# The residual addition of w_out: from a GpSimd addition and a store to an accumulating transfer onto x2 in DRAM

## The chip, the cores and the metric

The kernel runs on one core of one Trainium2 chip. A core has five instruction queues that run side by side: TensorE (PE; its weight loads are shown apart as PEld), VectorE (DVE), ScalarE (ACT), GpSimd (POOL) and SyncE (SP). SP only starts DMA transfers; here POOL starts a few of its own. Each queue runs its instructions strictly in the order in which they were laid down, and a wait for a semaphore holds everything behind it on that queue.

The metric is the device time of one execution in microseconds. The kernel before took 2776.52 us in the median of three runs (2768.33, 2776.52 and 2780.66).

## The reference

One layer of a streaming encoder for 2048 prompt rows and 8 × 16 rows of a second request group, with a model width of 1024. Cut to what the change touches:

```python
def rms_norm(x, g):
    y = x * lax.rsqrt(jnp.mean(x * x, axis=-1, keepdims=True) + EPS)
    return y * g

h = rms_norm(x, g0);  z = h @ w_in
A = band_attention(...)              # 8 heads x 64
B = mlstm(...)                       # 4 heads x 128
x = x + rms_norm(concat(rms_norm(A), sigmoid(o) * head_norm(B)) @ w_out)   # this line
x = x + rms_norm(conv_ffn(rms_norm(x)))                                    # w_up, conv, gelu gate, w_down
```

All of it is fp32. The marked line takes the mixed heads (rows × 1024), multiplies them by `w_out` (1024 × 1024), norms each row, scales by the row g1 and adds the layer's input x. Its result, called x2 below, is the input of the feed-forward block and of the last residual addition.

## The kernel before

**Tiling and stages.** The 2048 prompt rows are 16 tiles of 128 rows, and the second group, SAMPLE, is a 17th. The `w_in` product with attention and mLSTM runs up to about 1052 us, `w_out` from 1052 to 1323 us with the end of the attention mixed in, and then the feed-forward block in three parts of the hidden width (0, 1 and 2) up to 2778 us. x2 lives in DRAM, in one buffer `x2d[t]` per tile, and is read back three times: for the norm of the feed-forward block (`x2r`, L1079), and twice for later passes and the last addition (L1428, L1717).

**An fp32 product** is three matmuls of a rounded high part and a rest (`mm3`, L104 to L106): high·high, high·low, low·high. The parts come from a split: ScalarE casts the high part (L1309) and VectorE subtracts (L1310). `wu` are raw up-weights, `wuh` and `wul` their parts, `ws` sums of them.

**`project()`** (L968) does `w_out`, with the tiles in the order 0 to 7, SAMPLE, 8 to 15. For a tile t:

- `load` fetches the mixed heads into `mr` (L990). `norm` squares its attention half on ScalarE (L995), makes the row factor `att_rs` on POOL (L87, L93) and scales 128×512 on VectorE (L997); `turn_rows` transposes on TensorE (L76) and splits into `mt` on ScalarE and VectorE (L210, L211). All of that for tile t+1 is laid among the matmuls of tile t.
- `mx` is one tile of 2112 columns with the tag `wl`, of which there are two slots. `m` is its first 1024 columns, `xr` its second. SP loads x into `xr` (L1016).
- TensorE forms two halves `wo` of 512 columns (24 matmuls each), VectorE copies each out of PSUM into `m` (L1026), ScalarE squares it (L1028), and POOL makes the row factor `n_rs` (L87, L93).
- VectorE scales: `m = m · rs · g1` (L1038). POOL adds, `xr = m + xr` (L1039). SP stores `xr` to `x2d[t]` (L1040). When that store has landed, the slot is free.

The tag `wl` has other users: right after `project()`, the two slots of tiles 14 and 15 go to the low parts of the first up-weights (`wul`, written by VectorE at L1310). So VectorE's first `wul` waits for the store of tile 14.

**What sets the order.** The code is written as generators that are stepped in turn, so attention, mLSTM and `w_out` are laid down mixed. Then a scheduler with a simulated time line lays the instructions of each engine in a new order, and puts in the waits. An instruction in `tc.keep_in_program_order(...)` keeps its place on its engine relative to others so marked. Since the scheduler goes by its simulated times, a change in a few instructions can move many others.

Of the kernel before, what the change touches and what calls it, by code (L numbers as in the profile page):

```python
# [13 lines left out]
ALU = mybir.AluOpType  # L14
# [4 lines left out]
D = 1024  # L19
# [30 lines left out]
def hymba_step(ctx: ExitStack, tc: tile.TileContext, I: dict, O: dict):  # L50
    nc = tc.nc
# [8 lines left out]
    def ps_mm(name):  # L60
        return psum.tile([P, 512], F32, tag="mm", name=name)
# [10 lines left out]
    def dt_(shape, name):  # L72
        return dram.tile(shape, F32, tag=name, name=name)
# [12 lines left out]
    def mean_square(ms, ssq, n, eps=EPS):  # L86
        nc.gpsimd.tensor_scalar(ms, ssq, 1.0 / n, eps, op0=ALU.mult, op1=ALU.add)  # L87

    def rsqrt_mean(ssq, n, name, eps=EPS):
        ms = small.tile([P, 1], F32, tag="ms", name=name + "_ms")  # L90
        mean_square(ms, ssq, n, eps)
        rs = small.tile([P, 1], F32, tag="rs", name=name + "_rs")
        nc.gpsimd.tensor_tensor(rs, ms, nhalf[:, 0:1], op=ALU.pow)  # L93
        return rs
# [7 lines left out]
    def mm3(out, ah, al, bh, bl, start, stop, onto=False):  # L102

        nc.tensor.matmul(out, ah, bh, start=start, stop=False, skip_group_check=onto)  # L104
        nc.tensor.matmul(out, ah, bl, start=False, stop=False, skip_group_check=onto)  # L105
        nc.tensor.matmul(out, al, bh, start=False, stop=stop, skip_group_check=onto)  # L106
# [21 lines left out]
    x2d = [dt_([P, D], f"x2d{t}") for t in range(17)]  # L128

    def x_src(t):  # L130
        return I["x_sample"] if t == SAMPLE else I["x_prompt"][t * P:(t + 1) * P, :]
# [69 lines left out]
    def rows_to_T(hrow, chunk, j, name, bank):  # L201
        w = 4 if bank is not ps_big else KT
        for q in range(KT // w):
            pt = bank(f"{name}_pt{q}")
            for k in range(w):
                transpose(pt[:, k * P:(k + 1) * P], hrow[:, (w * q + k) * P:(w * q + k + 1) * P])
            ptv = pt.rearrange("p (k t) -> p k t", k=w)
            hv = chunk[:, 0, w * q:w * q + w, j * P:(j + 1) * P]
            lv = chunk[:, 1, w * q:w * q + w, j * P:(j + 1) * P]
            nc.scalar.copy(hv, ptv)  # L210
            nc.vector.tensor_tensor(lv, ptv, hv, op=ALU.subtract)  # L211
# [4 lines left out]
    def rows_tile(tag, shape, name, dtype=F32):  # L216
        if tag == "xr":
            return rows.tile(shape, dtype, tag="xr", name=name, bufs=2)
        return pa.tile(shape, dtype, tag=tag, name=name, bufs=1)
# [750 lines left out]
    def drain():  # L970
        while any([p_.step() for p_ in pipes]):
            pass

    def project(tiles):

        ss = [SimpleNamespace(t=t) for t in tiles]

        def load(s):
            t = s.t
            if t == 8:  # L980
                drain()
                open_ffn()
            s.m = rows_tile("xr", [P, D], f"mr{t}")
            if t == SAMPLE:
                for b in range(DB):
                    own = bass.AP(atts[b].tensor, atts[b].offset, [[512, DS], [DS * 512 + DA, HA], [1, DA]])
                    nc.sync.dma_start(s.m[b * DS:(b + 1) * DS, 0:512].rearrange("p (h d) -> p h d", h=HA), own)
                nc.sync.dma_start(s.m[:, 512:D], mixs)
            else:
                nc.sync.dma_start(s.m, mixd[t // 4][:, t % 4, :])  # L990

        def norm(s):
            mt = wpool.tile([P, 2112], F32R, tag="wh", name=f"mt{s.t}", bufs=2)
            ssq = small.tile([P, 1], F32, tag="ssq", name=f"assq{s.t}")
            nc.scalar.activation(mt[:, :512], s.m[:, :512], AF.Square, accum_out=ssq)  # L995
            rs = rsqrt_mean(ssq, 512, f"att{s.t}")
            nc.vector.tensor_scalar(s.m[:, :512], s.m[:, :512], rs, None, op0=ALU.mult)  # L997
            s.mt = mt[:, :2 * D].rearrange("p (a k n) -> p a k n", a=2, k=KT)

        def turn_rows(s):  # L1000
            rows_to_T(s.m, s.mt, 0, f"mT{s.t}", ps_mm if s.t < 8 else ps_big)

        load(ss[0])
        norm(ss[0])
        yield 0.0, 0.3
        turn_rows(ss[0])
        load(ss[1])
        yield 0.9, 1.2
        for n_, s in enumerate(ss):
            t = s.t  # L1010
            nxt = ss[n_ + 1] if n_ + 1 < len(ss) else None
            if nxt:
                norm(nxt)
            mx = wpool.tile([P, 2112], F32, tag="wl", name=f"mx{t}", bufs=2)
            m, xr = mx[:, 0:D], mx[:, D:2 * D]
            nc.sync.dma_start(xr, x_src(t))  # L1016
            for hf in range(2):
                c = slice(hf * 512, hf * 512 + 512)
                acc = ps_mm(f"wo{t}_{hf}")
                for k in range(KT):  # L1020
                    mm3(acc, s.mt[:, 0, k, :], s.mt[:, 1, k, :], wo[k][0][:, c], wo[k][1][:, c],
                        start=(k == 0), stop=(k == KT - 1))
                    if k % 4 == 3:
                        yield 2.6, 0.5
                ssq = small.tile([P, 1], F32, tag="wssq", name=f"wssq{t}_{hf}")
                nc.vector.tensor_copy(m[:, c], acc)  # L1026
                idle = m[:, 512:D] if hf == 0 else s.mt[:, 0, 0:4, :].rearrange("p k n -> p (k n)")
                nc.scalar.activation(idle, m[:, c], AF.Square, accum_out=ssq)  # L1028
                if hf == 0:
                    ssa = ssq  # L1030
                    mean_square(ssa, ssq, D)
                    if nxt:
                        turn_rows(nxt)
                        if n_ + 2 < len(ss):
                            load(ss[n_ + 2])
                        yield 0.9, 1.2
            rs = rsqrt_mean(ssq, D, f"n1_{t}", ssa)
            nc.vector.scalar_tensor_tensor(m, m, rs, g1[0], op0=ALU.mult, op1=ALU.mult)  # L1038
            nc.gpsimd.tensor_tensor(xr, m, xr, op=ALU.add)  # L1039
            nc.sync.dma_start(x2d[t], xr)  # L1040

# [5 lines left out]
    def open_ffn():  # L1049

        p1.close()
        ffn.p3 = ctx.enter_context(tc.tile_pool(name="p3", bufs=2, reuse_waits="tile"))
        ffn.halo = ffn.p3.tile([P, 44, 2], F32, tag="halo", name="halo", bufs=1)
        nc.vector.memset(ffn.halo, 0.0)
        ffn.g2 = ffn.p3.tile([P, D], F32, tag="g2", name="g2", bufs=1)
        nc.sync.dma_start(ffn.g2, I["norm_g"][2:3, :].broadcast_to([P, D]))
        pipes[:] = [Pipe(h2_units(0, lead=6)), Pipe(iter([]))]
# [187 lines left out]
    for n_, (half, gi) in enumerate(seq):  # L1245
# [22 lines left out]
        if n_ == len(seq) - 1:  # L1268
            out = project([0, 1, 2, 3, 4, 5, 6, 7, SAMPLE, 8, 9, 10, 11, 12, 13, 14, 15])
            split = w_out_steps()  # L1270
            next(split)
            next(out)
# [711 lines left out]
```

## Time and profile before

| | |
|---|---|
| Runs | 2768.33, 2776.52, 2780.66 us; median 2776.52 |
| Profiled execution | 2780.55 us |
| Its span, first to last instruction | 2778.8 us |
| Mean granted TensorE clock | 0.994 |
| TensorE busy | 2700.5 us (97%) |
| VectorE busy | 1971.7 us (71%) |
| ScalarE busy | 1439.6 us (52%) |
| GpSimd busy | 658.6 us (24%) |
| Moved by DMA | 532.52 MB, mean 192 GB/s |
| Stage `w_out`, 1052 to 1323 us: TensorE, VectorE, GpSimd busy | 265.76, 192.61, 101.94 of 271 us |

How to read it: the span runs from the first to the last instruction of one profiled execution, the time lies a little above it. Busy times of engines overlap. In the timeline each row has a start, a duration, the engine, the line of the code and the tiles `out<-in`; a bracket at the end tells for how long the engine had stood idle just before and whose end released it. A granted clock of 1.00 is TensorE's full speed.

### The profile page before, as it was taken

How to read it: one execution, taken by the hardware profiler on the slowest of the kernel's cores; microseconds unless marked ns; L12 is line 12 of the kernel's file. 1: busy time of each engine (PE TensorE's matmuls, PEld its weight loads, DVE VectorE, ACT ScalarE, POOL GpSimd, SP SyncE). 2: the span in 40 equal slices, each digit the busy share in tenths (PEclk: the TensorE clock that was granted, in tenths of full speed). 3: DMA queues.
4: the chain of work that ended last, by engine and by line, in shares of the span. 5: the costliest groups of instructions: out<-in, count | busy, mean ns of one | idle time of the engine just before them, and what ended most of it. 6: DMA issues, size and time to landing. Idle time of an engine off the chain costs nothing.

```text
span 2778.8 us, 47788 instructions
## 1 busy us (share of the span) xinstructions
PE 2700.5 (97%) x16422; PEld 2525.1 (91%) x16422; DVE 1971.7 (71%) x3637; ACT 1439.6 (52%) x2918; POOL 658.6 (24%) x1249
## 2 busy tenths in 40 slices
PE   7999999999999999999999999999999999999998
PEld 7899999998899998878999998789999778989976
DVE  5244455645546668766989987668998866999966
ACT  4355555634346666543555455445455665545554
POOL 1000010211100002335433322123442112555301
PEclk9999999999999999999999999999999999999999
DMA  5534355556564456345645559866775766777775
GB/s 182 157 116 139 105 164 168 163 152 211 156 184 141 136 169 196 107 163 195 230 153 188 167 183 329 301 224 198 225 225 170 250 223 231 216 236 231 233 268 183
DMA packets 322850, 532.52 MB, mean 192 GB/s; under 512 B 59650, under 2 KB 156638, under 8 KB 322478
## 3 DMA queue, kind: packets, MB, share of 16 engines
q1 hardware_dynamic: 251838, 400.11, 46.6%
q0 software_dynamic: 25840, 83.98, 7.9%
q10 hardware_dynamic: 44928, 45.37, 5.0%
q8 instruction: 129, 2.11, 0.3%
q14 instruction: 115, 0.94, 0.1%
HBM read 383.28 MB, written 149.18 MB: 192 GB/s over the span
## 4 chain that ended last, share of the span: by engine, by line
PE 49%; DVE 5%; DMA 3%; issue 2%; ACT 1%; POOL 1%; SPq 0%; DVEq 0%; POOLq 0%; ACTq 0%
PE uec L104 5%; PE uec L105 5%; PE uec L106 5%; PE dn L106 4%; PE dn L105 3%; PE dn L104 3%; PE ua L106 3%; PE ua L105 3%; PE ua L104 3%; PE wo L106 2%; PE wo L104 2%; PE wo L105 2%; PE dnm L105 1%; PE dnm L106 1%; PE dnm L104 1%
## 5 line engine op out<-in xcount | busy, mean ns | idle before, releaser
L104 PE MATMUL uec<-B,wuh 128*128 128x384 f32 (+1 forms) x720 | 237.8, 331 | 11.8 <-DVE uu L1642 10.7
L105 PE MATMUL uec<-B,wuh 128*128 128x384 f32 (+1 forms) x720 | 236.5, 328 | 0.0
L106 PE MATMUL uec<-B,wul 128*128 128x384 f32 (+1 forms) x720 | 234.8, 328 | 0.0
L1309 ACT CAST wuh<-wu 128x512 fp32r<-128x512 f32 x255 | 141.4, 618 | 112.4 <-PE uec L105 105.4
L1310 DVE TENSOR_TENSOR wul<-wu,wuh 128x512 fp32r<-128x512 f32 x255 | 170.4, 703 | 4.0 <-DMA x2d<-mx 2.8
L405 DVE CUSTOM_DVE_ANT_0 tmp<-s,nb 128x640 f32<-128x640 f32 (+4 forms) x128 | 94.4, 738 | 95.6 <-PE s L395 94.2
L104 PE MATMUL vo<-wi_h,hT 128*128 128x256 f32 x544 | 155.2, 285 | 0.8 <-DVE mt L211 0.6
L106 PE MATMUL vo<-wi_h,hT 128*128 128x256 f32 x544 | 155.6, 286 | 0.0
L105 PE MATMUL vo<-wi_l,hT 128*128 128x256 f32 x544 | 154.8, 285 | 0.0
L104 PEld LDWEIGHTS uec<-B,wuh 128*128 128x128 f32 x720 | 136.2, 189 | 15.3 <-DVE uu L1642 12.4
L104 PE MATMUL qk<-hT,wi_h 128*128 128x384 f32 (+1 forms) x384 | 130.3, 339 | 7.4 <-ACT qk_st L236 4.1
L105 PEld LDWEIGHTS uec<-B,wuh 128*128 128x128 f32 x720 | 136.4, 189 | 0.2
L106 PEld LDWEIGHTS uec<-B,wul 128*128 128x128 f32 x720 | 136.2, 189 | 0.0
L1506 ACT ACTIVATE y<-y 128x768 f32<-128x768 f32 (+1 forms) x66 | 53.8, 815 | 155.5 <-DVE y L1504 155.5
L418 DVE TENSOR_TENSOR ptl<-pt,pth 128x640 fp32r<-128x640 f32 (+4 forms) x128 | 93.7, 738 | 56.5 <-ACT pth L417 55.5
L406 ACT ACTIVATE tmp<-tmp,mn 128x640 f32<-128x640 f32 (+4 forms) x128 | 97.6, 762 | 64.2 <-DVE mn L405 62.4
L1310 DVE TENSOR_TENSOR wdl<-wdr,wdh 128x512 fp32r<-128x512 f32 x198 | 124.9, 686 | 7.0 <-ACT wdh L1309 6.8
L105 PE MATMUL qk<-hT,wi_h 128*128 128x384 f32 (+1 forms) x384 | 128.9, 336 | 0.0
L106 PE MATMUL qk<-hT,wi_l 128*128 128x384 f32 (+1 forms) x384 | 128.5, 335 | 0.0
L1310 DVE TENSOR_TENSOR al<-ar,ah 128x768 fp32r<-128x768 f32 (+2 forms) x94 | 71.1, 765 | 80.9 <-ACT ah L1309 80.7
L105 PE MATMUL qb<-hT,wi_h 128*128 128x384 f32 (+1 forms) x384 | 127.9, 333 | 0.0
L106 PE MATMUL qb<-hT,wi_l 128*128 128x384 f32 (+1 forms) x384 | 127.2, 331 | 0.0
(443 smaller groups left out, 9443.9 us busy)
## 6 DMA issues: line engine op xcount, KB each, us to landing
wu<-in_w_up SPq DMA_DIRECT2D x220, 256.0 KB, 4.4
wu<-wsd SPq DMA_DIRECT2D x176, 256.0 KB, 4.1
wdr<-in_w_down SPq DMA_DIRECT2D x110, 256.0 KB, 5.8
wi_raw<-in_w_in SPq DMA_DIRECT2D x52, 512.0 KB, 4.0
wsd<-ws POOLq DMA_DIRECT2D x88, 256.0 KB, 3.7
wdr<-wtd SPq DMA_DIRECT2D x88, 256.0 KB, 4.8
gr<-gd SPq DMA_DIRECT2D x39, 384.0 KB, 5.9
kraw<-kTd SPq DMA_DIRECT2D x112, 128.0 KB, 3.2
```

Of the source, the lines that this page charges most:

```text
L104: nc.tensor.matmul(out, ah, bh, start=start, stop=False, skip_group_check=onto)
L105: nc.tensor.matmul(out, ah, bl, start=False, stop=False, skip_group_check=onto)
L106: nc.tensor.matmul(out, al, bh, start=False, stop=stop, skip_group_check=onto)
L405: nc.vector.tensor_tensor_reduce(o_, s_, b_, 1.0, 3e38, ALU.add, ALU.min, accum_out=mn)
L406: nc.scalar.activation(tmp[:, :n], tmp[:, :n], AF.Exp, bias=mn, scale=-1.0, accum_out=rsum[:, i % 4, hh:hh + 1])
L418: nc.vector.tensor_tensor(s.ptl[:, sl, qc], ptv, s.pth[:, sl, qc], op=ALU.subtract)
L1309: nc.scalar.copy(h, r)
L1310: nc.vector.tensor_tensor(l, r, h, op=ALU.subtract)
L1506: nc.scalar.activation(y[:, :ln], y[:, :ln], AF.Gelu_apprx_tanh)
```

## The change

The second half of `mx` is no longer used. At the start of a tile's loop SP copies x from its input straight into `x2d[t]`, in DRAM; this copy is marked to keep its place in SP's order. After VectorE's scaling there is no addition on POOL and no store on SP. Instead POOL starts one DMA transfer that adds `m`, as it lies in SBUF, onto `x2d[t]` (`accum_op=ALU.add`). It waits for the scaling and for the copy. The slot of `mx` is free when this transfer has landed, and the readers of `x2d[t]` wait for it too.

```diff
             mx = wpool.tile([P, 2112], F32, tag="wl", name=f"mx{t}", bufs=2)
-            m, xr = mx[:, 0:D], mx[:, D:2 * D]
-            nc.sync.dma_start(xr, x_src(t))
+            m = mx[:, 0:D]
+            tc.keep_in_program_order(nc.sync.dma_start(x2d[t], x_src(t)))
             for hf in range(2):
...
             rs = rsqrt_mean(ssq, D, f"n1_{t}", ssa)
             nc.vector.scalar_tensor_tensor(m, m, rs, g1[0], op0=ALU.mult, op1=ALU.mult)
-            nc.gpsimd.tensor_tensor(xr, m, xr, op=ALU.add)
-            nc.sync.dma_start(x2d[t], xr)
+            nc.gpsimd.dma_start(x2d[t], m, accum_op=ALU.add)
```

Line numbers of the new kernel are the old ones up to L1038, and one less behind it. SP has 1445 rows before and 1428 now; POOL has as many as before. The other engines have the same instructions as before, in an order that differs from the end of the attention to the first part of the feed-forward block.

On POOL, around the end of tile 9 (`n1_9_rs` is that tile's row factor, `att11_rs` that of the heads of tile 11, `mx9` its slot), before:

```order
L93 TENSOR_TENSOR n1_9_rs_15547<-n1_9_ms_15545,nhalf_77 128x1
L87 TENSOR_SCALAR att11_ms_15555<-assq11_15553 128x1
L93 TENSOR_TENSOR att11_rs_15557<-att11_ms_15555,nhalf_77 128x1
L1039 TENSOR_TENSOR mx9_15455<-mx9_15455 128x1024
L87 TENSOR_SCALAR wssq10_0_15606<-wssq10_0_15606 128x1
```

and now:

```order
L93 TENSOR_TENSOR n1_9_rs_15537<-n1_9_ms_15535,nhalf_77 128x1
L87 TENSOR_SCALAR att11_ms_15544<-assq11_15542 128x1
L93 TENSOR_TENSOR att11_rs_15546<-att11_ms_15544,nhalf_77 128x1
L1039 DMA x2d9_289<-mx9_15445 128x1024
L87 TENSOR_SCALAR wssq10_0_15595<-wssq10_0_15595 128x1
```

The transfer stands in the place of the addition, between the row factor of the next tile's heads and the next tile's mean square.

On VectorE, at the end of `w_out` (`wo14_1` is the second half of tile 14, `wul0_0_0` the first up-weights' low part, in a slot that `mx14` had), before:

```order
L1026 COPY mx14_16018<-wo14_1_16060 128x512
L1038 SCALAR_TENSOR_TENSOR mx14_16018<-mx14_16018,n1_14_rs_16090,norm_row1_13117 128x1024
L1026 COPY mx15_16095<-wo15_0_16097 128x512
L1310 TENSOR_TENSOR wul0_0_0_16167<-wu0_0_16168,wuh0_0_0_16166 128x512
L1310 TENSOR_TENSOR wul0_0_0_16167<-ws0_1_16177,wuh0_0_0_16166 128x512
L1310 TENSOR_TENSOR wul0_0_0_16167<-ws0_2_16178,wuh0_0_0_16166 128x512
L1310 TENSOR_TENSOR wul0_0_0_16167<-ws0_0_16176,wuh0_0_0_16166 128x512
L1326 TENSOR_TENSOR ws1_0_16239<-wu1_3_16237,wu1_2_16235 128x512
L1026 COPY mx15_16095<-wo15_1_16126 128x512
```

and now:

```order
L1026 COPY mx14_16003<-wo14_1_16045 128x512
L1325 TENSOR_TENSOR ws0_1_16160<-ws0_0_16159,wu0_0_16151 128x512
L1325 TENSOR_TENSOR ws0_2_16161<-wu0_0_16151,wu0_3_16157 128x512
L1325 TENSOR_TENSOR ws0_3_16162<-wu0_1_16153,ws0_1_16160 128x512
L1026 COPY mx15_16079<-wo15_0_16081 128x512
L1038 SCALAR_TENSOR_TENSOR mx14_16003<-mx14_16003,n1_14_rs_16075,norm_row1_13117 128x1024
L1026 COPY mx15_16079<-wo15_1_16110 128x512
L1309 TENSOR_TENSOR wul0_0_0_16150<-wu0_0_16151,wuh0_0_0_16149 128x512
L1309 TENSOR_TENSOR wul0_0_0_16150<-ws0_1_16160,wuh0_0_0_16149 128x512
```

The scaling of tile 14 now stands behind the first evacuation of tile 15, and the first `wul` behind the second evacuation of tile 15; the sums `ws0`, which stood further ahead, stand between the evacuations.

On SP at the same place, before (`lated` are late parts of the feed-forward block's input; `B3` reads them), in part:

```order
L1040 DMA x2d12_292<-mx12_15784 128x1024
L1016 DMA mx14_16018<-in_x_prompt 128x1024
L1115 DMA lated1_277<-b212_15994 512x1x128
L1321 DMA wu0_0_16168<-in_w_up 128x512
L1115 DMA lated2_278<-t42_15996 512x1x128
L1321 DMA wu0_1_16170<-in_w_up 128x512
L1321 DMA wu0_2_16172<-in_w_up 128x512
L1321 DMA wu0_3_16174<-in_w_up 128x512
L1040 DMA x2d13_293<-mx13_15904 128x1024
L1321 DMA wu1_0_16231<-in_w_up 128x512
L1321 DMA wu1_1_16233<-in_w_up 128x512
L1016 DMA mx15_16095<-in_x_prompt 128x1024
```

and now:

```order
L1114 DMA lated1_277<-b212_15980 512x1x128
L1320 DMA wu0_0_16151<-in_w_up 128x512
L1114 DMA lated2_278<-t42_15982 512x1x128
L1016 DMA x2d14_294<-in_x_prompt 16x8192
L1016 DMA x2d15_295<-in_x_prompt 16x8192
L1320 DMA wu0_1_16153<-in_w_up 128x512
L1320 DMA wu0_2_16155<-in_w_up 128x512
L1320 DMA wu0_3_16157<-in_w_up 128x512
L1320 DMA wu1_0_16214<-in_w_up 128x512
L1320 DMA wu1_1_16216<-in_w_up 128x512
```

No store stands between the weight loads any more, and the copies of x for the last two tiles stand together ahead of them.

## The prediction

> **What bounds the kernel now.** I read the head of the page first, then the windows of the stage that changes, what TensorE waits for there, and last the rows of the edited lines.
>
> ```profile
> span 2778.8 us, 47788 instructions
> PE 2700.5 (97%) x16422; PEld 2525.1 (91%) x16422; DVE 1971.7 (71%) x3637; ACT 1439.6 (52%) x2918; POOL 658.6 (24%) x1249
> ```
>
> TensorE is busy for 97% of the span. What any other engine saves counts only where TensorE has a gap. The `w_out` stage runs from 1052 to 1323 us, and the hand-over to the feed-forward block takes the next 23 us (columns: window, its length, then busy us of PE, PEld, DVE, ACT and POOL, granted clock, DMA share, GB/s):
>
> ```profile
> 1052.00:1323.00 271.00, 265.76 (x1424) 222.79 (x1423) 192.61 (x302) 132.55 (x315) 101.94 (x137) 0.99 0.50 163
> 1323.00:1346.00 23.00, 20.80 (x118) 19.90 (x117) 22.18 (x28) 14.10 (x21) 8.11 (x9) 1.00 0.70 267
> 1346.00:1680.00 334.00, 331.85 (x1860) 323.93 (x1859) 306.40 (x467) 171.18 (x278) 115.48 (x196) 1.00 0.55 183
> ```
>
> TensorE is idle for 271.00 − 265.76 = 5.2 us in the stage, 2.2 us in the hand-over and 2.2 us in the 334 us behind it. That is the whole visible purse. From 1052 to 1346 us its gaps end as follows (total, times, longest):
>
> ```profile
> PE pt L76 <- DVE ptl L418: 1.8, 1, 1.8
> PE ua L106 <- DVE wul L1310: 1.6, 1, 1.6
> PE ub L106 <- DVE wu L1310: 0.6, 1, 0.6
> PE ot L431 <- DVE ptl L418: 0.5, 1, 0.5
> PE wo L104 <- DVE mt L211: 0.4, 1, 0.4
> ```
>
> Every one is VectorE being late; neither the additions nor the stores of x2d end a gap.
>
> **The change, part by part.** The groups of the edited lines, and of one line beside them (duration in ns min/median/max, then first and last start):
>
> ```profile
> L1039 POOL TENSOR_TENSOR mx<-mx x17: 2373/2394/2575, 1077.2 to 1329.5; 128x1024 f32<-128x1024 f32 x17
> L1040 SPq DMA_DIRECT2D x2d<-mx x17: 319/326/397, 1079.6 to 1332.1; - x17
> L1016 SPq DMA_DIRECT2D mx<-in_x_prompt x16: 327/338/567, 1052.3 to 1310.3; - x16
> L997 DVE TENSOR_SCALAR mr<-mr,att_rs x17: 482/2604/2621, 1013.0 to 1304.1; 128x512 f32<-128x512 f32 x17
> ```
>
> *Removed: 17 additions on POOL.* 17 × 2.394 = 40.7 us of POOL. POOL is busy 102 of 271 us in the stage and ends no TensorE gap, so this by itself is 0. But look at L997: the same 128x512 scaling takes 0.48 us at least and 2.60 us in the median. The timeline shows which:
>
> ```profile
> 1175.47 2.39 POOL L1039 TENSOR_TENSOR mx<-mx 128x1024 f32<-128x1024 f32 x1
> 1175.53 2.61 DVE L997 TENSOR_SCALAR mr<-mr,att_rs 128x512 f32<-128x512 f32 x1 [0.71 <-POOL att_rs L93]
> 1178.66 0.81 DVE L405 CUSTOM_DVE_ANT_0 tmp<-s,nb 128x640 f32<-128x640 f32 x1
> 1181.58 0.83 DVE L418 TENSOR_TENSOR ptl<-pt,pth 128x640 fp32r<-128x640 f32 x1 [0.30 <-ACT pth L417]
> 1182.46 0.77 PE L76 MATMUL pt<-ident,tmp 128*128 128x128 f32 x5 [1.80 <-DVE ptl L418]
> ...
> 1240.13 0.49 DVE L997 TENSOR_SCALAR mr<-mr,att_rs 128x512 f32<-128x512 f32 x1 [0.71 <-POOL att_rs L93]
> ```
>
> The scaling that starts beside the addition at 1175.47 ends with it (1178.14 against 1177.86); the one at 1240.13, with no addition beside it, takes 0.49. So more than half of the 17 lose 2.1 us of VectorE each. Behind the long one stand the softmax's L405 and L418, and behind those the longest gap, 1.80. Without the block L405 could start about 1.4 us earlier (the evacuation between them then waits for its product for part of the 2.1). The clock columns show what such a gap costs besides:
>
> ```profile
> 1184.00:1188.00 4.00, 4.00 (x13) 3.22 (x12) 2.12 (x5) 1.60 (x5) 0.00 (x0) 0.63 0.19 79
> 1188.00:1192.00 4.00, 4.00 (x24) 3.41 (x23) 0.00 (x0) 0.00 (x0) 0.00 (x0) 1.00 0.02 4
> ```
>
> Right after it the granted clock is 0.63 for 4 us: 13 matmuls, against 24 in the next 4 us. 4 × (1 − 0.63) = 1.5 us. The gaps of 0.54 and 0.41 stand at 1160.99 and 1164.68, behind
>
> ```profile
> 1156.73 2.62 DVE L997 TENSOR_SCALAR mr<-mr,att_rs 128x512 f32<-128x512 f32 x1 [0.71 <-POOL att_rs L93]
> ```
>
> The gain is 1.4 + 1.5 + 0.5 + 0.4 = 3.8 us. Bounds: nothing, if a later link of the chain (ScalarE's exponentials) is the true limit; 5.2 + 1.5 = 6.7, if every gap of the stage goes.
>
> *Removed and added on SP.* 17 loads (0.34 each) and 17 stores (0.33) go, 17 copies of x come: one issue per tile fewer, 17 × 0.33 = 5.5 us of SP. SP's waits shrink more:
>
> ```profile
> SPq L1040 <- POOL mx L1039: 91.0, 15, 19.6
> SPq L1016 <- DMA x2d<-mx: 27.2, 12, 2.9
> ```
>
> The store's 91.0 us in line ahead of later loads move to POOL, the load's 27.2 us of waiting for the slot go. No gap of TensorE in the list ends with a load, so I take 0; a weight that arrives sooner has no one waiting for it. Cover gone, the price would be at most the 2.9 us of one such wait. The copies are pinned in SP's order, wait for no buffer, and stand a tile ahead of the accumulation that needs them. They add a read and a write that replace the load's read and the store's write; the accumulation adds 512 KB read and 512 KB written per tile: 17 MB over 271 us is 66 GB/s on 163. In the hand-over the share of the DMA engines is 0.70 already, which lengthens landings there.
>
> *Added on POOL: 17 accumulating transfers.* No row shows one. Issuing and landing are bounded by the nearest rows:
>
> ```profile
> L1328 POOL DMA_DIRECT2D wsd<-ws x88: 539/539/760, 1309.2 to 1621.7; - x88
> x2d<-mx SPq DMA_DIRECT2D x17, 512.0 KB, 3.0
> x2r<-x2d SPq DMA_DIRECT2D x17, 512.0 KB, 6.0
> wsd<-ws POOLq DMA_DIRECT2D x8, 256.0 KB, 6.5
> ```
>
> The issue costs POOL 0.54 in place of 2.39 and waits where the addition waited, for VectorE's scaling (and for the copy); behind it on POOL are the next tile's mean squares, which come sooner. Landing L: 3.0 is the plain store, a floor; two landings one after the other, 6.0 + 6.5 = 12.5, are my ceiling. I take 6.0, nearest to the row of the same 512 KB out of x2d and to POOL's own transfers in these microseconds.
>
> [...]
>
> *Moved: who frees the slot.* `mx` has two slots, so tile 15 needs tile 13's.
>
> ```profile
> 1302.10 1.28 DVE L1038 SCALAR_TENSOR_TENSOR mx<-mx,n_rs,norm_row 128x1024 f32<-128x1024 f32 x1 [1.00 <-POOL n_rs L93]
> 1317.44 0.69 DVE L1026 COPY mx<-wo 128x512 f32<-128x512 f32 x1 [1.73 <-PE wo L106]
> 1318.22 0.33 SPq L1040 DMA_DIRECT2D x2d<-mx  x1
> 1320.97 0.69 DVE L1310 TENSOR_TENSOR wul<-wu,wuh 128x512 fp32r<-128x512 f32 x1 [2.83 <-DMA x2d<-mx]
> 1323.89 0.34 PE L106 MATMUL ua<-B,wul 128*128 128x384 f32 x1
> ```
>
> The scale of tile 13 ends at 1303.4, tile 15's first evacuation starts at 1317.44: 14 us for L, so 0 by L = 6.0. At the end the cover is thinner. Tile 14's slot goes to `wul`, the first up-weights; VectorE already waits 2.83 us for the store there, and TensorE needs `wul` at 1323.89. In the new order tile 14's scaling stands behind tile 15's first evacuation, so it ends at 1317.44 + 0.69 + 1.28 = 1319.4; then L, then 0.69: 1319.4 + 6.0 + 0.7 = 1326.1, a gap of about 2.2 us. Ends: L = 3.0 gives none by this (about 0.6, since tile 15's second evacuation, for a matmul that ends at 1323.0, now also precedes `wul`); L = 12.5 gives 8.7. A gap of 1.80 cost 1.5 by the clock, one of 1.6 (in the hand-over, clock 1.00) nothing: half, 0.7. Together +2.9 (0.6 to 10.2).
>
> *Moved: the rest.* The scheduler re-laid matmuls, splits and evacuations from the attention tail through the first block. Each place can be better or worse; the nearest measure is the 2.2 us of gaps in the 334 us behind, so 0, with ends of −4 and +4 (two gaps of about 2 us either way).
>
> **Sum.** −3.8 + 2.9 + 0 = −0.9 on the profiled execution's 2780.55 (its span is 2778.8): 2779.65. That execution is 4.0 above the median of the runs, 2776.52; taken over, 2776 us (2775.6, rounded).
>
> **Rivals.** *Accumulations land too late (slower).* With L above 14 us the two slots bind. For: no row shows an accumulating transfer, and it reads DRAM and writes it back. Against: 3.0 to 6.5 in the rows. At L = 20 each slot's round, two tiles long, grows by up to 6 us, 3 us per tile over the 15 tiles that reuse a slot, up to 45; the end adds 16. With attention work filling a part, about +50: 2826. It decides from about L = 15: 15 × 0.5 for the slots, 11.2 at the end, 0.7, less 3.8, is 15.6, over the 14 us that can be told.
>
> *The new order stalls TensorE (slower).* The moved rows, not the transfer: VectorE is busy 22.18 of 23 us in the hand-over and 306 of 334 behind it, so work put ahead of a split is felt at once. Against: as many rows moved forward as back. Six more gaps of 1.8 with the clock's 1.5: 6 × 3.3 = 20 us, 2796.
>
> *VectorE freed is worth more (faster).* If the 2.1 us blocks also cost TensorE time that shows as busy, all gaps go and some hidden time: 7.4 + 1.5 + some 6 us, about −15: 2761. Against: TensorE already covers most of the dozen blocks without a gap.
>
> *The change doesn't do what it says.* If POOL's transfer waited for a late copy, or its issue cost as much as the addition, VectorE would be blocked as before: gain 0, end +2.9, 2779.4. SP's order puts the copies well ahead, so I give it little and count it under no change.
>
> **How the numbers follow.** About 0.5%, 14 us, is what a measurement of this kernel can tell from no change. My forecast, with the case just named, has 0.67 (own range 2768 to 2788); late landing 0.10; the new order 0.17; more than the gaps 0.06. So faster 0.06, same 0.67, slower 0.27. The range is 2764 to 2806: it takes in the terms' ends (−6.7 + 0.6 − 4 and 10.2 + 4), and half of the slower cases; beyond it lie about 0.15 above and 0.04 below.
>
> **What would show it.** L997 at 0.48 us in nearly all 17; no POOL addition, 17 issues near 0.54; the 1.80 gap and the 0.63 clock behind it gone; landing of the accumulations near 6 us; VectorE's first `wul` waiting for that landing, and a TensorE gap of about 2 us at 1324. Wrong would be: landings over 15 us, with evacuations L1026 waiting for them; or the same landings and many new gaps in the attention tail or the first block.

## The result and the profile after

The changed kernel takes 2795.49 us in the median of six runs, against 2777.97 for six of the kernel before: a ratio of 1.0072 (95% interval 1.0057 to 1.0087), 17.5 us slower. The forecast was "no change", 2776; the range (2764 to 2806) holds the time, the direction was missed. The profiled execution of the changed kernel took 2806.41 us, the longest of the six, so its rows are read for what waits for what, and a second profile of the same kernel (2794.17 us, the first experiment) for what comes back.

The head of the page, changed kernel:

```profile
span 2804.7 us, 47744 instructions
PE 2712.3 (97%) x16422; PEld 2535.2 (90%) x16422; DVE 1940.9 (69%) x3637; ACT 1438.0 (51%) x2918; POOL 634.1 (23%) x1249
```

VectorE and POOL did get lighter, by 31 and 24 us, and TensorE is still busy for 97%. The groups that answer to the edited lines, and L997 beside them:

```profile
L1039 POOL DMA_DIRECT2D x2d<-mx x17: 878/917/1081, 1078.7 to 1341.9; - x17
L1016 SPq DMA_DIRECT2D x2d<-in_x_prompt x16: 499/618/1266, 1055.2 to 1307.5; - x16
L997 DVE TENSOR_SCALAR mr<-mr,att_rs x17: 480/486/523, 1014.1 to 1308.7; 128x512 f32<-128x512 f32 x17
DMA to landing us min/median/max: 5.4/6.1/11.3
```

(The last line is that of the accumulating transfers.) VectorE's blocks are gone: all 17 scalings take 0.48 to 0.52 us. The median landing is 6.1 us, as forecast. What was not forecast, in size or at all, are these waits of TensorE from 1320 to 1860 us, the three longest:

```profile
PE ua L106 <- DVE wul L1309: 8.3, 1, 8.3
PE dnm L104 <- ACT gh L1308: 7.5, 4, 4.6
PE h2T_pt L1106 <- ACT b L1123: 2.0, 1, 2.0
```

**First place, the hand-over at 1323 us.** The timeline of POOL, VectorE and TensorE around tile 14:

```profile
1321.52 0.43 POOL L87 TENSOR_SCALAR n_ms<-wssq,wssq 128x1 f32<-128x1 f32 x1
1321.90 1.15 POOL L1327 DMA_DIRECT2D wsd<-ws  x2
1322.02 0.69 DVE L1026 COPY mx<-wo 128x512 f32<-128x512 f32 x1 [0.20 <-PE wo L106]
1323.06 0.58 POOL L93 TENSOR_TENSOR n_rs<-n_ms,nhalf 128x1 f32<-128x1 f32 x1
1323.68 1.29 DVE L1038 SCALAR_TENSOR_TENSOR mx<-mx,n_rs,norm_row 128x1024 f32<-128x1024 f32 x1 [0.96 <-POOL n_rs L93]
...
1325.27 0.94 POOL L1039 DMA_DIRECT2D x2d<-mx  x1 [0.25 <-DVE mx L1038]
...
1336.67 0.69 DVE L1309 TENSOR_TENSOR wul<-wu,wuh 128x512 fp32r<-128x512 f32 x1 [8.29 <-DMA x2d<-mx]
...
1337.42 0.69 PE L106 MATMUL ua<-B,wul 128*128 128x384 f32 x1 [8.30 <-DVE wul L1309]
```

VectorE is idle for 0.96 us ahead of tile 14's scaling: it waits for the row factor `n_rs`, which POOL makes 1.54 us after the mean square `n_ms`, because two transfers of weight sums (`wsd`) stand between them; in the kernel before the two rows are 0.34 us apart (1313.49 and 1313.83). Tile 14's transfer starts at 1325.27 and VectorE goes on at 1336.67: 11.4 us. In the same microseconds SP sends the four late parts of the block's input, 768 KB each:

```profile
1324.15 4.28 SPq L1163 DMA_DIRECT2D B<-lated  x4
```

The windows of the changed kernel behind that (window, length, busy us of PE, PEld, DVE, ACT and POOL, then granted clock, share of the DMA engines and GB/s):

```profile
1329.00:1333.00 4.00, 0.12 (x1) 0.00 (x0) 0.00 (x0) 1.79 (x5) 0.82 (x2) 0.99 1.03 300
1333.00:1337.00 4.00, 0.00 (x0) 0.00 (x0) 0.33 (x1) 0.00 (x0) 0.00 (x0) 0.50 1.01 377
1337.00:1341.00 4.00, 3.58 (x11) 3.58 (x12) 4.00 (x7) 0.00 (x0) 0.33 (x1) 0.50 0.26 102
1341.00:1345.00 4.00, 4.00 (x18) 4.00 (x18) 2.88 (x5) 3.98 (x5) 2.28 (x4) 0.73 0.55 176
```

The DMA engines are full, 1.03 and 1.01, while TensorE stands still. The clock is 0.50 when it goes on, and 0.73 for 4 us more, which costs another 4 × 0.50 + 4 × 0.27 = 3.1 us.

**Second place, the end of the feed-forward's first block, 340 us later.** No line of the diff is there. The timeline of ScalarE in the kernel before:

```profile
1658.56 1.03 ACT L1502 ACTIVATE y<-ug,wcv 128x768 f32<-128x768 f32 x1
1659.50 1.76 ACT L1309 CAST gh<-gr 128x384 fp32r<-128x384 f32 x4
1662.86 1.06 ACT L1095 ACTIVATE B<-x2r 128x1024 fp32r<-128x1024 f32 x1 [1.61 <-DMA x2r<-x2d]
...
1668.02 1.06 ACT L1095 ACTIVATE B<-x2r 128x1024 fp32r<-128x1024 f32 x1 [1.63 <-DMA x2r<-x2d]
```

and in the changed kernel, with one row of TensorE:

```profile
1670.21 1.06 ACT L1094 ACTIVATE B<-x2r 128x1024 fp32r<-128x1024 f32 x1 [5.77 <-DMA x2r<-x2d]
...
1673.34 1.03 ACT L1501 ACTIVATE y<-ug,wcv 128x768 f32<-128x768 f32 x1
1674.27 1.74 ACT L1308 CAST gh<-gr 128x384 fp32r<-128x384 f32 x4
...
1687.99 1.06 ACT L1094 ACTIVATE B<-x2r 128x1024 fp32r<-128x1024 f32 x1 [6.36 <-DMA x2r<-x2d]
...
1691.63 0.83 ACT L1308 CAST gh<-gr 128x768 fp32r<-128x768 f32 x1
...
1692.51 0.80 PE L104 MATMUL dnm<-wdh,gh 128*128 128x512 f32 x1 [4.55 <-ACT gh L1308]
```

The first `B<-x2r` (the square for the next block's norm) now stands ahead of the gate's `y` and of the splits `gh`, and waits 5.77 us for its load in place of 1.61. What stands behind it comes late; SP sends the second x2r load late in turn (at 1679.99, after a wait for VectorE's `y`), the second `B<-x2r` waits 6.36, and the splits that TensorE needs stand behind that one. TensorE's gap of 4.55 is followed by the clock's drop, and so is a second stretch of gaps 90 us later (windows of the changed kernel):

```profile
1690.00:1700.00 10.00, 7.49 (x21) 5.94 (x22) 6.32 (x9) 3.96 (x7) 0.69 (x2) 0.66 0.91 322
...
1780.00:1790.00 10.00, 8.90 (x31) 7.09 (x32) 9.30 (x17) 7.67 (x18) 5.42 (x11) 0.66 0.65 247
```

**How much at each place.** From windows of 20 us I added up the counts of TensorE's matmuls, and read (between two windows, in proportion) when the 7500th, the 9000th and so on had started, in each kernel's profile and in that of the kernel before. The growth of the difference from the 7500th to the 9000th (1071 to 1353 us before) is the loss in `w_out` with the hand-over, from the 10500th to the 11500th (1612 to 1828 us) that at the end of the first block. All are against one profile of the kernel before, and stretches in which no row moved differ by up to 5 us between profiles, so only large entries mean something.

| Kernel | `w_out` and hand-over, us | End of block, us | Ratio to before (95%) |
|---|---|---|---|
| changed | 13.0 | 14.2 | 1.0072 (1.0057 to 1.0087) |
| changed, again | 9.6 | 13.8 | 1.0052 (1.0033 to 1.0071) |
| tiles 14 and 15 old | 0.9 | 1.3 | 0.9999 (0.9987 to 1.0011) |
| before, with copies | 0.9 | 0.3 | 1.0001 (0.9991 to 1.0010) |
| before, no addition | −1.5 | 1.8 | 0.9987 (0.9974 to 1.0000) |
| tile 15 old | 6.3 | 1.7 | 1.0028 (1.0018 to 1.0038) |
| other buffer | 9.2 | 14.2 | 1.0058 (1.0043 to 1.0073) |
| plain transfers | 8.6 | 12.1 | 1.0054 (1.0034 to 1.0074) |
| only 14 and 15 new | −0.6 | 10.0 | 1.0044 (1.0029 to 1.0059) |
| not pinned | 0.0 | −0.4 | 1.0100 (1.0076 to 1.0125) |
| not pinned, two old | −1.1 | 0.9 | 1.0079 (1.0063 to 1.0095) |
| copy half a tile later | 10.5 | 0.5 | 1.0039 (1.0025 to 1.0053) |
| copy two tiles earlier | 2.9 | 0.3 | 1.0006 (0.9993 to 1.0018) |

The two unpinned kernels lose 22 to 26 us in the first 100 us. The experiments follow in the order in which they were run.

### The profile page after: what moved, and what is told of

The parts are those of the page before. It is cut to its first block, busy times and chain, and to the rows that moved or that the text cites. A ratio compares the mean times of both kernels' runs of the same rounds, so it can differ in the third digit from the quotient of the medians.

```text
span 2804.7 us, 47744 instructions
## 1 busy us (share of the span) xinstructions
PE 2712.3 (97%) x16422; PEld 2535.2 (90%) x16422; DVE 1940.9 (69%) x3637; ACT 1438.0 (51%) x2918; POOL 634.1 (23%) x1249
## 4 chain that ended last, share of the span: by engine, by line
PE 43%; DMA 3%; DVE 3%; issue 2%; ACT 1%; POOL 1%; SPq 0%; ACTq 0%; DVEq 0%; POOLq 0%
PE uec L104 6%; PE uec L105 6%; PE uec L106 6%; PE dn L106 3%; PE dn L105 3%; PE dn L104 3%; PE ua L106 3%; PE ua L105 3%; PE ua L104 3%; PE ub L106 1%; PE ub L105 1%; PE ub L104 1%; PE dnm L104 1%; PE dnm L106 1%; PE dnm L105 1%
```

## The experiments

Each edit is against the changed kernel unless it says otherwise. The theory after the first comparison: two costs, the wait for tile 14's accumulation at the hand-over, and the moved rows at the end of the first block. The rivals: everything is order; everything follows from the late `wul`; the accumulating transfer itself costs time wherever it stands.

**The changed kernel again** (no edit).

> The changed kernel once more, for a second profile beside the others. If the gap of 8.30 us at the first wul, which waits for tile 14's accumulation, belongs to the kernel, it is here again within 1 us, with the granted clock low behind it; time 2790 to 2798. If the two clock drops between 1680 and 1790 us belong to the order, they are here again; if they were chance, this profile has other ones and the time is nearer 2790.

2793.97 us. TensorE's gaps from 1323 to 1350, and from 1350 to 1900 us:

```profile
PE ua L106 <- DVE wul L1309: 7.3, 1, 7.3
...
PE dnm L104 <- ACT gh L1308: 5.3, 3, 4.7
PE h2T_pt L1106 <- ACT b L1123: 5.2, 1, 5.2
```

Both places come back, with the clock low behind them (0.50 from 1324 to 1332 us and 0.76 for 4 us more; 0.83 from 1680 to 1700 us), so they belong to the kernel. Of the 12 us by which the first profile was longer, some 5 lie ahead of the 7500th matmul and some 3 in `w_out` with the hand-over; they did not come back.

**Tiles 14 and 15 undone.**

```diff
-            m = mx[:, 0:D]
-            tc.keep_in_program_order(nc.sync.dma_start(x2d[t], x_src(t)))
+            m, xr = mx[:, 0:D], mx[:, D:2 * D]
+            if t in (14, 15):
+                nc.sync.dma_start(xr, x_src(t))
+            else:
+                tc.keep_in_program_order(nc.sync.dma_start(x2d[t], x_src(t)))
...
-            nc.gpsimd.dma_start(x2d[t], m, accum_op=ALU.add)
+            if t in (14, 15):
+                nc.gpsimd.tensor_tensor(xr, m, xr, op=ALU.add)
+                nc.sync.dma_start(x2d[t], xr)
+            else:
+                nc.gpsimd.dma_start(x2d[t], m, accum_op=ALU.add)
```

> Tiles 14 and 15 alone go back to the load of x, the POOL addition and the SP store; the other 15 tiles accumulate as in the changed kernel. Theory (the end: the first wul waits for an accumulation that lands late): the gap at the first wul falls from 8.3 to under 2.5 us, the clock behind it stays at 1.00, and the time falls by about 10 us against the changed kernel, to about 2786. Rival (the moved rows of w_out cost it): those rows up to the end of w_out stand as in the changed kernel, so the time stays above 2790.

2778.82 us against 2778.57 for the kernel before: the whole loss is gone, more than expected, because the order of the first block went back to the old one too. TensorE has no gap at the first `wul`; a later `wul`, some 17 us on, has one of 1.6, as in the kernel before (at 1342.62 and 1341.01). And VectorE's blocks stay away (L997 takes 0.49 us in the median, 0.53 at most), without the kernel being faster than the one before. So freeing VectorE is not worth its 3.8 us here: TensorE's idle time from 1052 to 1323 us is 271.00 − 263.67 = 7.3 us, 5.2 before, and its longest waits there have other names:

```profile
PE h2T_pt L1113 <- DVE x2r L1105: 2.4, 3, 0.9
PE wo L106 <- DVE mt L211: 2.0, 3, 1.1
PE ot L430 <- ACT pth L417: 1.1, 1, 1.1
```

**The kernel before, with the copies alone.** The edit is against the kernel before.

```diff
+            tc.keep_in_program_order(nc.sync.dma_start(x2d[t], x_src(t)))
             nc.sync.dma_start(xr, x_src(t))
```

> The kernel before with nothing but the 17 pinned copies of x onto x2d added; the later stores overwrite them. All four computing engines keep their order row by row. Both theories: within 3 us of the kernel before, 2775 to 2781, since neither SP nor DRAM ends a gap. If the copies or their place in SP's order cost time (the rival that the DMA traffic does it), 5 us or more above the kernel before.

1.0001. The copies and their place in SP's order cost nothing while the other engines' rows stand as before.

**The kernel before, without the POOL additions.** Against the kernel before.

```diff
-            nc.gpsimd.tensor_tensor(xr, m, xr, op=ALU.add)
-            nc.sync.dma_start(x2d[t], xr)
+            nc.sync.dma_start(x2d[t], m)
```

> The kernel before without the 17 POOL additions: m is stored without x, the loads of x stay. It leaves out the residual addition. It measures what freeing POOL and VectorE is worth without any accumulation: L997 at 0.49 us in all 17. By the sum of the prediction 3.8 us faster than before, about 2774; by the rival that VectorE's free time is covered by TensorE's own work, within 1.5 us of before; by the rival that the block also costs hidden time, 10 us or more faster.

2776.76 us, 1.8 us under the kernel before, with an interval from 0 to 7 us. That takes in the 3.8 as well as the second alternative, and this run does not tell them apart.

**Tile 15 alone undone.** The edit of tiles 14 and 15 with `t == 15`.

> Tile 15 alone goes back to load, POOL addition and store; tile 14 still accumulates, and its slot still goes to the first wul. Behind the hand-over all rows stand as in the kernel with tiles 14 and 15 undone. Theory of two costs (the wait for tile 14's accumulation, about 9 us; and rows of the first block put in another order, about 12 us): a gap of 5 to 9 us at the first wul with a low clock behind it, no loss between 1600 and 1860, about 2787. Rival (all follows from the late wul, which throws the later rows off): the loss between 1600 and 1860 comes too, 2793 or more. Rival (all is order): no gap, 2779.

2786.00 us: the end of the block is well (1.7), and `w_out` with the hand-over loses 6.3. But not as expected: in this order tile 14's transfer starts at 1318.21, ahead of the late parts (1323.91), and VectorE waits 1.28 us for it. The loss is another wait, VectorE for a weight load, with tile 15's rows `mt` behind it (timeline of VectorE):

```profile
1310.38 0.69 DVE L1332 TENSOR_TENSOR ws<-wu,wu 128x512 f32<-128x512 f32 x1 [6.78 <-DMA wu<-in_w_up]
```

**m of tiles 14 and 15 in another buffer.**

```diff
-            mx = wpool.tile([P, 2112], F32, tag="wl", name=f"mx{t}", bufs=2)
+            if t in (14, 15):
+                mx = row(f"mx{t}")
+            else:
+                mx = wpool.tile([P, 2112], F32, tag="wl", name=f"mx{t}", bufs=2)
```

> All 17 tiles accumulate as in the changed kernel, but m of tiles 14 and 15 lies in a row buffer of the feed-forward block, so that wul's slots come free with tiles 12 and 13. The rows from 1400 us to the end of the second block stand exactly as in the changed kernel. Theory of two costs: no wait for an accumulation at the first wul, the loss between 1600 and 1860 with its clock drops is here all the same (12 us or so), about 2789. Rival (all follows from the late wul): no loss there either, about 2779.

2794.18 us. No `wul` waits for an accumulation, and the end of the block still loses 14.2 (`gh` 6.5, `b` 5.5 us of gaps). So the second cost doesn't follow from the late `wul`. (The hand-over as a whole is still 9.2 us late here. That lateness is not the cause either: two kernels below lose at one of the two places and not at the other.) The hand-over stayed dear here by another wait, TensorE for the late part's split, 3.7 us.

**Plain transfers.**

```diff
-            nc.gpsimd.dma_start(x2d[t], m, accum_op=ALU.add)
+            nc.gpsimd.dma_start(x2d[t], m)
```

> The changed kernel with plain transfers in place of the accumulating ones, from the same POOL queue; every row of every engine stands as in the changed kernel. It leaves out the residual addition. If accumulation as such makes the landing long (a read and an add more), the median landing falls from 6.1 to about 4 us, that of tile 14 from 11 to about 6, the gap at wul from 8 to about 3 us, and the time by 5 to 9 us. If the load on the DMA engines at that place makes it (weights, the late parts B and the sums wsd land there too), tile 14's landing stays at 9 us or more and the time at 2790 to 2797.

2795.29 us, with all rows as in the changed kernel. The group of the transfers, and their landing:

```profile
L1039 POOL DMA_DIRECT2D x2d<-mx x17: 539/683/757, 1076.6 to 1334.7; - x17
DMA to landing us min/median/max: 3.0/4.3/10.6
```

TensorE's gaps at the two places:

```profile
PE ua L106 <- DVE wul L1309: 3.5, 1, 3.5
...
PE dnm L104 <- ACT gh L1308: 5.6, 3, 4.0
```

This tells two things apart. Accumulating costs 6.1 − 4.3 = 1.8 us of landing in the median, 5.4 − 3.0 = 2.4 between the shortest, and 0.23 us of issue; at tile 14 the transfer takes 7.7 us from its issue to VectorE's `wul` (1321.86 to 1329.54) against 11.4 and 10.7, and the gap is 3.5 against 8.3 and 7.3. And the end of the block loses 12.1 us without any accumulation, so that loss is the order's. The time did not fall by the 5 to 9 us expected: the median is that of the changed kernel, over a wide spread (2784.68 to 2800.87). Of the 8.6 us in the table 3.8 come ahead of the hand-over, between the 7500th and the 8000th matmul.

**Only tiles 14 and 15 new.** The edit of tiles 14 and 15, with `t not in (14, 15)`.

> The complement: only tiles 14 and 15 accumulate, the other 15 load, add and store as before. Up to the end of w_out the rows stand as in the kernel before, so POOL blocks VectorE there as before; behind it they stand nearly as in the changed kernel. If the whole loss lies with the last two tiles (the wait and the rows moved by it), the time is that of the changed kernel, 2790 to 2798, with both the gap at wul and the loss between 1600 and 1860. If the 15 others share in it, 2787 or less.

2789.24 us, in between: the end of the block loses 10.0, `w_out` with the hand-over nothing. Up to `w_out`'s end its rows are the old ones, so tile 14 is scaled before tile 15's evacuation, its transfer starts at 1312.12, 3.5 us ahead of the burst of late parts, and `wul` starts 6.7 us later:

```profile
1312.12 0.95 POOL L1046 DMA_DIRECT2D x2d<-mx  x1 [1.63 <-DVE mx L1041]
1318.86 0.69 DVE L1316 TENSOR_TENSOR wul<-wu,wuh 128x512 fp32r<-128x512 f32 x1 [4.62 <-DMA x2d<-mx]
```

The accumulation of tile 14 alone is thus not dear; it is dear where it falls into the burst. (No run moves the burst alone; this compares orders.)

**The copies not kept at their place.**

```diff
-            tc.keep_in_program_order(nc.sync.dma_start(x2d[t], x_src(t)))
+            nc.sync.dma_start(x2d[t], x_src(t))
```

> The changed kernel with the copies of x not kept at their place: the scheduler lays all 17 near the head of SP's order. In the first block ScalarE's rows then stand as in the kernel before (the down-weight splits behind gh of the fifth step), while at the hand-over tile 14's scaling and the first wul stand as in the changed kernel. Theory of two costs: a gap of 4 to 8 us at the first wul, no loss between 1600 and 1860, about 2787, if the early copies cost nothing at the start. Rival (the accumulations disturb the first block by themselves): the loss between 1600 and 1860 is there, 2793 or more.

2805.28 us, for a reason of its own: the scheduler puts the 17 copies at the head of SP's order (10.0 to 33.2 us), where TensorE waits for its first inputs, and some 25 us are lost by the 500th matmul. Its first window:

```profile
0.00:40.00 40.00, 20.83 (x115) 19.47 (x116) 14.79 (x25) 13.65 (x21) 5.00 (x23) 0.90 0.97 336
```

The DMA engines are full (0.97) and TensorE runs 115 matmuls; in the kernel before it runs 216 in that window, with the DMA engines at 0.70. Behind that, neither place loses anything (0.0 and −0.4), though all 17 tiles accumulate. The expectation was mistaken in one thing: in this order tile 14's scaling stands ahead of tile 15's evacuation, as in the kernel before, so the gap at `wul` is 0.5 us.

**The same with tiles 14 and 15 undone.** Both edits together.

> The same with tiles 14 and 15 gone back to load, addition and store: neither cost is left, VectorE is free of the POOL additions in 15 tiles. Theory: 2775 to 2780, the time of the kernel before, since the gaps that the free VectorE closes are replaced by others. If the pinned copies held something back on SP that the gain of 3.8 us needs, 2774 or less, faster than both kernels.

2800.44 us: 22 us at the start, nothing behind it. The expectation forgot the start.

**The pinned copy half a tile later.**

```diff
-            tc.keep_in_program_order(nc.sync.dma_start(x2d[t], x_src(t)))
...
                 if hf == 0:
+                    tc.keep_in_program_order(nc.sync.dma_start(x2d[t], x_src(t)))
                     ssa = ssq
```

> The whole change, all 17 tiles accumulate, but the pinned copy stands one half tile later: behind the evacuation of the tile's first half instead of at the start of its loop. The scheduler's rows of the first block then stand as in the kernel before; the hand-over stands as in the changed kernel (tile 14's scaling behind tile 15's first evacuation, the first wul last). Theory (order alone decides each cost): the wait at the first wul and its gap of 5 to 8 us are here, the loss between 1600 and 1860 isn't; 2783 to 2788. Rival (accumulation itself costs it): as the changed kernel, 2791 or more.

2788.45 us, 10 us over the kernel before: the gap at `wul` is here alone. Its gaps from 1320 to 1360 us, the longest of them:

```profile
PE ua L106 <- DVE wul L1309: 7.4, 1, 7.4
```

There is no gap of `dnm` from 1600 to 1870 us.

**The pinned copy two tiles earlier.**

```diff
                 nc.sync.dma_start(s.m, mixd[t // 4][:, t % 4, :])
+            tc.keep_in_program_order(nc.sync.dma_start(x2d[t], x_src(t)))
...
-            tc.keep_in_program_order(nc.sync.dma_start(x2d[t], x_src(t)))
```

> The whole change, all 17 tiles accumulate, but the pinned copy stands two tiles earlier, behind the load of the tile's mixed heads. Here both places stand as in the kernel before: tile 14's scaling ahead of tile 15's first evacuation, and ScalarE's rows of the first block in the old order. Theory (order alone decides each cost): no gap over 2.5 us at the first wul, no loss between 1600 and 1860, 2775 to 2781, the kernel before within 0.15%. Rival (accumulation itself costs time, wherever it stands): 2785 or more. If the freed POOL and VectorE are worth the 3.8 us of the prediction in this order, 2774 or less.

2778.94 us against 2778.46, a ratio of 1.0006. The whole change costs nothing that these runs can tell in this order (the interval is −1.9 to +5.0 us). The timeline of VectorE, TensorE and ScalarE at the two places:

```profile
1311.49 0.69 DVE L1325 TENSOR_TENSOR ws<-wu,wu 128x512 f32<-128x512 f32 x1 [6.38 <-DMA wu<-in_w_up]
1315.31 0.80 PE L106 MATMUL wo<-wo,mt 128*128 128x512 f32 x1 [3.98 <-DVE mt L211]
1317.72 1.28 DVE L1038 SCALAR_TENSOR_TENSOR mx<-mx,n_rs,norm_row 128x1024 f32<-128x1024 f32 x1 [1.88 <-POOL n_rs L93]
1323.13 0.69 DVE L1026 COPY mx<-wo 128x512 f32<-128x512 f32 x1 [4.13 <-PE wo L106]
1325.19 0.69 DVE L1309 TENSOR_TENSOR wul<-wu,wuh 128x512 fp32r<-128x512 f32 x1 [1.36 <-DMA x2d<-mx]
...
1670.99 1.06 ACT L1094 ACTIVATE B<-x2r 128x1024 fp32r<-128x1024 f32 x1 [2.28 <-DMA x2r<-x2d]
```

Tile 14 is scaled ahead of tile 15's evacuation, VectorE waits 1.36 us for the transfer, and ScalarE 2.28 us for x2r. There is one other stop, as with tile 15 alone undone: VectorE waits 6.38 us for a weight load, tile 15's rows `mt` come behind that, and TensorE stands still for 3.98 us, with a granted clock of 0.84 over the window from 1300 to 1320 us. So the 2.9 us in the table have a cause of their own. The kernel does not beat the one before, and no run here tries whether it would without that stop.

## Why the prediction was wrong, point by point

- **VectorE freed (−3.8).** The mechanism was right: L997 is 0.47 to 0.53 without an addition beside it. The size did not show: 1.8 us (0 to 7) without the additions, which leaves 3.8 possible, and nothing (0.9999, 1.0006) in the two accumulating kernels in a good order, which have new gaps of their own. The clock's price of a gap, 1.5 us, was counted as a gain, while new gaps of the same kind can pay it too. The list of gaps in the prediction leaves out one of 0.3 us that waits for ScalarE; it changes nothing in the sum.
- **SP and the copies (0).** Right at the place where they were put, with all other rows as before (1.0001). A copy costs SP 0.62 us to start, against 0.34 for a load, so SP saves hardly anything where 5.5 us were expected; nothing waited for that. The traffic was estimated at 66 GB/s more in the stage; its window shows 156 GB/s, against 163 before, and a DMA share of 0.59 against 0.50. Far ahead of their use, at the kernel's start, the copies cost 22 to 26 us.
- **POOL's issue (0.54).** It is 0.92, hidden as was said.
- **Landing (6.0) and the end of `w_out` (+2.9, to 10.2).** The median of 6.1 is right; the failed part is that one landing time, nearest to the median, was used for tile 14. Its landing was 11 us, since the transfer fell into the late parts' burst; in four kernels where it starts ahead of the burst VectorE goes on after 5.5 to 6.7 us. The cover was well estimated: from the end of the scaling to TensorE's need 4.5 us by the prediction's rows, 4.2 measured. But the evacuation ahead of the scaling is not what held the scaling up in the profile: that was POOL's row factor. The gap is 8.3 and 7.3 us where 2.2 was taken; 8.7 was named as the end of the range. The clock behind it cost some 3 us where 0.7 was taken. In the kernel with the copy half a tile later this place is the only one left, and the kernel is 10 us slower.
- **The moved rows (0, ends −4 and +4).** This is the step that failed most: it was set to 0 from the gaps that the old order has there, and it cost 14 us at the end of the first block. The chain through the x2r loads is read from the timeline and not tried apart; that the rows' order costs it is shown by four kernels that have that order and lose 10 to 14 us there, one without the wait at `wul` and one without accumulation, and by those without that order, which lose under 2.
- **The rivals.** "The new order stalls TensorE" was the right one. Its number, 2796, came out within 1 us of the median by luck: a few long gaps in place of six short ones, and one of them is a late landing. It was given 0.17, though about a thousand of TensorE's rows had moved. Late landing did not bind the slots in the stage: the median is 6.1 against 14 us to spare.

The two costs together with the rest do not add up exactly in one profile: 13.8 and 9.6 us at the two places, against 15.4 us between the medians. The difference, about 8 us, is spread over stretches in which rows did not move, and stays within what two profiles of one kernel differ by.

## What to carry to other kernels

When a scheduler lays the order anew, an edit of three lines costs first what the new order costs, and that can come hundreds of microseconds behind the edit: compare the order row by row where an engine waits for a load with splits behind it, and price that place from the timeline. A variant that moves one pinned instruction by half a tile or by two tiles tells the cost of the edit from the cost of the order (here 0.0006 against 0.0039 and 0.0072). And a transfer whose landing frees a buffer must be timed in the traffic at that moment, not by its median.

## What the runs showed of the hardware

An accumulating transfer of 512 KB from SBUF onto DRAM lands in 6.1 us in the median and 5.4 at the least, a plain one from the same queue in 4.3 and 3.0 us; GpSimd spends 0.92 and 0.68 us on starting it. Among four transfers of 768 KB (a DMA share of 1.03 and 1.01 in the changed kernel's windows from 1329 to 1337 us), the same two take 11.4 and 7.7 us until VectorE goes on; the accumulating one takes 5.5 to 6.7 us where it starts ahead of those four.

After TensorE had stood still for 8.3 us the granted clock was 0.50 over 4 us and 0.73 over the next 4. The 10 us in which the gap of 4.55 us ended (1690 to 1700 us), and the 10 us behind a window with 3.45 us of gaps (1780 to 1790 us), show 0.66. The gap of 1.80 us in the kernel before was followed by 0.63 over 4 us: in this kernel a gap of 2 us can already cost the clock. It need not: behind TensorE's wait of 1.94 us for `uu`, which ends at 2433.72 us in the kernel before and at 2463.15 in the changed one, the clock stayed at 1.00 in both. In each of the other 12 profiles I took the first window of 20 us behind 2420 us with 2.1 to 2.3 us of TensorE idle: five show 1.00 there and in the window behind it, and seven show 0.91 to 0.96 in at least one of the two, among them the changed kernel's second profile (0.91). So the clock's price of such a gap can't be read from one profile, and two profiles of one kernel can differ by it.
